# A fused add and layer norm on one core: sums kept in the residual's ring, loops over fixed rows, branch hints, a new transfer order

## The chip, the cores and the metric

The kernel runs on 1 core of one Trainium2 chip. The metric is the device time of one execution in microseconds (us), lower is better. The kernel before takes 238.18 us (median of 3 runs, 238.14 to 238.33). "Span" is what the profile covers of a run, about 1.3 us less than the time.

## The reference

```python
# x, residual: 16 x 1024 x 512, float32; gamma, beta: 512
z = x + residual
mean = np.mean(z, axis=-1, keepdims=True)
var = np.var(z, axis=-1, keepdims=True)
return gamma * (z - mean) / np.sqrt(var + eps) + beta
```

Every element is read twice (x and residual) and written once: 67.11 MB in, 33.55 MB out. The arithmetic is small. In the kernel's words there are 128 "rows": one row is a tile of 128 partitions x 512 elements, 2 KB in each partition.

## The kernel before

Four engines form a pipeline. SyncE issues every large transfer, in the order of a written PLAN, on one queue. GpSimd adds x and residual. ScalarE makes two passes (mean, then sum of squares) and a square root. VectorE makes two passes (add the mean and multiply by gamma; multiply by 1/std and add beta) and a reciprocal between them. x and the result live in a ring of 64 rows (`zbuf`), residual in a ring of 32 rows (`rbuf`). ScalarE and VectorE work in turns of 4 rows.

```python
PLAN = """
x0+8 r0+8 x8+8 r8+8 x16+16 r16+16 x32+16 r32+16
x48+16 r48+16 o0+16 r64+16 x64+16 o16+16 r80+16 x80+16
o32+16 r96+16 x96+8 x104+8 o48+16 r112+16 x112+8 x120+8
o64+16 o80+16 o96+16 o112+12 o124+4
"""                            # r48+16: residual rows 48 to 63; o: a store
ADDS = [4, 4, 8] * 7 + [4] * 4
# ...
for kind, lo, n in moves:      # SyncE, in the order of PLAN
    if kind == "x":
        # ... waits until the store that used these rows of zbuf has landed
    elif kind == "r":
        wait_rows(s_add, "add", lo + n - R_ROWS)   # ring free once ADDED
    else:
        wait_rows(s_out, "out", lo + n)
# GpSimd
z = part(zbuf, Z_ROWS, lo, n)
nc.gpsimd.tensor_tensor(out=z, in0=z, in1=part(rbuf, R_ROWS, lo, n), op=ALU.add
                        ).then_inc(s_add, n)
# ScalarE: 16 laps of 2 turns, addresses from registers
with act.Fori(0, total // LAP) as lap:
    z0 = act.snap((lap * (LAP * D)) % (Z_ROWS * D))
    # ... per turn: wait for the adds, 4 x Identity with accum_out (mean),
    #     4 x Square with accum_out, one Sqrt
# VectorE: 16 laps of 2 turns
    dve.wait_ge(s_ssq, due)    # 4 x (z + nm) * gamma, then wait for std,
                               # reciprocal, 4 x z * rstd + beta
```

Of the kernel before, what the change touches and what calls it, by code (L numbers as in the profile page):

```python
# [8 lines left out]
FP32 = mybir.dt.float32  # L9
ACT = mybir.ActivationFunctionType  # L10
ALU = mybir.AluOpType
# [3 lines left out]
Z_ROWS = 64  # L15
R_ROWS = 32


PLAN = """
x0+8 r0+8 x8+8 r8+8 x16+16 r16+16 x32+16 r32+16  # L20
x48+16 r48+16 o0+16 r64+16 x64+16 o16+16 r80+16 x80+16
o32+16 r96+16 x96+8 x104+8 o48+16 r112+16 x112+8 x120+8
o64+16 o80+16 o96+16 o112+12 o124+4
"""


ADDS = [4, 4, 8] * 7 + [4] * 4


TURN = 4  # L30
SETS = 2
LAP = SETS * TURN


EARLY = 2
# [3 lines left out]
def kernel(  # L39
# [9 lines left out]
    nc = tc.nc  # L49
    P = nc.NUM_PARTITIONS  # L50
# [3 lines left out]
    N, D = xf.shape  # L54
    inv_d = 1.0 / float(D)
    total = N // P
# [16 lines left out]
    def dram(t, lo, n):  # L73

        b0 = lo - lo % BLOCK
        v = t[P * b0 : P * (b0 + BLOCK), :].rearrange("(p j) d -> p j d", p=P)
        return v[:, lo - b0 : lo - b0 + n, :].rearrange("p a b -> p (a b)")

    zbuf = nc.alloc_sbuf_tensor("zbuf", [P, Z_ROWS * D], FP32)
    rbuf = nc.alloc_sbuf_tensor("rbuf", [P, R_ROWS * D], FP32)  # L80
# [1 line left out]
    ones = nc.alloc_sbuf_tensor("ones", [1, P], FP32)  # L82
    eps_t = nc.alloc_sbuf_tensor("eps_t", [P, 1], FP32)
    nm, ssq, std, rstd = (
        [nc.alloc_sbuf_tensor(f"{name}{j}", [P, TURN], FP32) for j in range(SETS)]
        for name in ("nm", "ssq", "std", "rstd")
    )
    gamma_p = nc.alloc_psum_tensor("gamma_p", [P, D], FP32)
    beta_p = nc.alloc_psum_tensor("beta_p", [P, D], FP32)
# [8 lines left out]
    def sem(name):  # L98
        s = nc.alloc_semaphore(name)
        sems.append(s)  # L100
        return s
# [4 lines left out]
    s_gb = [sem(f"gb{k}") for k in range(2)]  # L106
    s_const = sem("const")
    s_pe = sem("pe")
    s_add = sem("add")

    s_mean, s_ssq, s_std = sem("mean"), sem("ssq"), sem("std")
    s_dve = sem("dve")
    s_out = sem("out")
    so = [sem(f"so{c}") for c in range(len(stores))]
    nums = [s.num for s in sems]
# [2 lines left out]
    def part(buf, size, lo, n):  # L118
        assert lo % size + n <= size
        return buf[:, (lo % size) * D : (lo % size + n) * D]  # L120
# [13 lines left out]
        ).then_inc(s_pe, 1)  # L134


    seen = {"add": 0, "out": 0}
    first = []

    def wait_rows(s, key, rows):  # L140
        if rows > seen[key]:
            nc.sync.wait_ge(s, rows)
            seen[key] = rows

    def move(out, in_, s):
        i = nc.sync.dma_start(out=out, in_=in_).then_inc(s, 16)  # L146
        if len(first) < EARLY:
            first.append(i.ins)

    gone = 0  # L150
    for kind, lo, n in moves:
        if kind == "x":
            while gone < len(stores) and stores[gone][0] < lo + n - Z_ROWS:
                nc.sync.wait_ge(so[gone], 16)
                gone += 1
            move(part(zbuf, Z_ROWS, lo, n), dram(xf, lo, n), sx[loads_x.index((lo, n))])
        elif kind == "r":
            wait_rows(s_add, "add", lo + n - R_ROWS)
            move(part(rbuf, R_ROWS, lo, n), dram(rf, lo, n), sr[loads_r.index((lo, n))])
        else:  # L160
            wait_rows(s_out, "out", lo + n)
            move(dram(of, lo, n), part(zbuf, Z_ROWS, lo, n), so[stores.index((lo, n))])


# [8 lines left out]
    lo = 0  # L173
    for n in ADDS:
        for key, loads, s in (("x", loads_x, sx), ("r", loads_r, sr)):
            while landed[key] < len(loads) and loads[landed[key]][0] < lo + n:
                nc.gpsimd.wait_ge(s[landed[key]], 16)  # L177
                landed[key] += 1
        z = part(zbuf, Z_ROWS, lo, n)
        nc.gpsimd.tensor_tensor(  # L180
            out=z, in0=z, in1=part(rbuf, R_ROWS, lo, n), op=ALU.add
        ).then_inc(s_add, n)
        lo += n
    assert lo == total




    act = nc.scalar
    act.preload_act_table_set("sqrt_and_others")  # L190
    act.wait_ge(s_const, 2)
    act.sem_inc(s_dve, LAP)
    with act.Fori(0, total // LAP) as lap:  # L193
        z0 = act.snap((lap * (LAP * D)) % (Z_ROWS * D))
        r0 = act.snap(lap * LAP)
        for j in range(SETS):
            due = act.snap(r0 + (j + 1) * TURN)
            act.wait_ge(s_dve, due)
            act.wait_ge(s_add, due)
            zk = [zbuf[:, bass.ds(z0 + (j * TURN + k) * D, D)] for k in range(TURN)]  # L200
            for k in range(TURN):
                i = act.activation(  # L202
                    out=junk_m[k][:, :],
                    in_=zk[k],
                    func=ACT.Identity,
                    scale=-inv_d,
                    accum_out=nm[j][:, k : k + 1],
                )
            i.then_inc(s_mean, TURN)
            act.wait_ge(s_mean, due)  # L210
            for k in range(TURN):
                i = act.activation(  # L212
                    out=junk_s[k][:, :],
                    in_=zk[k],
                    func=ACT.Square,
                    bias=nm[j][:, k : k + 1],
                    accum_out=ssq[j][:, k : k + 1],
                )
            i.then_inc(s_ssq, TURN)
            act.wait_ge(s_ssq, due)  # L220
            act.activation(  # L221
                out=std[j][:, :],
                in_=ssq[j][:, :],
                func=ACT.Sqrt,
                bias=eps_t[:, 0:1],
                scale=inv_d,
            ).then_inc(s_std, TURN)


    dve = nc.vector  # L230
    dve.wait_ge(s_pe, 2)
    with dve.Fori(0, total // LAP) as lap:
        z0 = dve.snap((lap * (LAP * D)) % (Z_ROWS * D))
        r0 = dve.snap(lap * LAP)
        for j in range(SETS):
            due = dve.snap(r0 + (j + 1) * TURN)
            zk = [zbuf[:, bass.ds(z0 + (j * TURN + k) * D, D)] for k in range(TURN)]
            dve.wait_ge(s_ssq, due)
            for k in range(TURN):
                dve.scalar_tensor_tensor(  # L240
                    out=zk[k],
                    in0=zk[k],
                    scalar=nm[j][:, k : k + 1],
                    in1=gamma_p[:, :],
                    op0=ALU.add,
                    op1=ALU.mult,
                )
            dve.wait_ge(s_std, due)
            dve.reciprocal(out=rstd[j][:, :], in_=std[j][:, :]).then_inc(s_dve, TURN)  # L249
            dve.wait_ge(s_dve, due + LAP)  # L250
            for k in range(TURN):
                i = dve.scalar_tensor_tensor(  # L252
                    out=zk[k],
                    in0=zk[k],
                    scalar=rstd[j][:, k : k + 1],
                    in1=beta_p[:, :],
                    op0=ALU.mult,
                    op1=ALU.add,
                )
            i.then_inc(s_out, TURN)  # L260


    blks = nc.main_func.blocks
# [43 lines left out]
```

## Time and profile before

The first thing to ask is which resource never rests. The page's busy view cuts the span into 40 slices; a digit is the busy share in tenths, 9 is 90% or more.

```profile
DVE  0001977939699999999898989896989895698920
ACT  2019879497999999999999998979998956999300
POOL 0098920999799699604995059944995049950000
DMA  8999999999999999999999999999999999999996
```

The DMA row has 9 everywhere but in the first and the last slice. The table of DMA queues (packets, MB, share of 16 engines' span) says the same in one number, and shows one instruction fetch:

```profile
q1 hardware_dynamic: 4176, 100.67, 99.2%
q14 instruction: 1, 0.01, 0.0%
```

The chain of work that ended last, by engine, is mostly DMA:

```profile
DMA 71%; POOL 9%; ACT 9%; DVE 2%; issue 2%; SPq 1%; ACTq 0%; DVEq 0%; POOLq 0%
```

The groups of instructions (count | busy us, mean ns | idle before, and what ended it) show that the compute engines wait:

```profile
L180 POOL TENSOR_TENSOR zbuf<-zbuf,rbuf 128x2048 f32<-128x2048 f32 (+1 forms) x25 | 142.8, 5740 | 67.6 <-DMA zbuf<-in_x_dram 40.8
L240 DVE SCALAR_TENSOR_TENSOR zbuf<-zbuf,nm,gamma_p 128x512 f32 x128 | 87.1, 743 | 46.3 <-ACT junk_s L212 46.3
L202 ACT ACTIVATE junk_m<-zbuf 128x512 f32 x128 | 74.9, 585 | 29.1 <-POOL zbuf L180 27.5
```

The waits of the queue that issues (SyncE; us in total, times, longest) tell what each transfer's issue hangs on. Here residual loads wait for GpSimd's adds (the first line):

```profile
SPq L146 <- POOL zbuf L180: 94.0, 6, 27.6
SPq L146 <- DMA out_dram<-zbuf: 74.0, 4, 21.0
SPq L146 <- DVE zbuf L252: 46.0, 3, 22.0
```

These waits cost nothing by themselves. What matters is whether the queue still holds issued work when they end. The view of DMA issues (count, KB each, median us from issue to landing) shows that it does: a 4 MB residual load lands 30.5 us after its issue, although the queue lands a 4 MB transfer every 9.7 us (the median engine reports one at 31.49 us and the next at 41.21); it queues behind others.

```profile
rbuf<-in_residual_dram SPq DMA_DIRECT2D x7, 4096.0 KB, 30.5
```

From the timeline of SyncE (start us, duration), the issues of residual rows 32 and 48, and of the last store:

```profile
31.01 0.33 SPq L146 DMA_DIRECT2D rbuf<-in_residual_dram  x1
...
59.41 0.33 SPq L146 DMA_DIRECT2D rbuf<-in_residual_dram  x1
...
226.67 0.33 SPq L146 DMA_DIRECT2D out_dram<-zbuf  x1
```

Where do the 236.9 us of the span go, then? The trace has a record of every DMA packet. A packet of 32 KB (one partition's 16 rows) typically takes 1,213 ns, one of 16 KB 611 ns, one of 8 KB 309 ns. Summed at these values, an engine's data packets take 233.2 us (total of all packets, divided by 16). 16 packets of 32 KB in 1,213 ns are 432 GB/s; what sets this rate is not shown.

### The profile page before, as it was taken

The page shows a single profiled execution, that of the slowest core. Times are in us where ns is not written, and L with a number is a line of the kernel's source. Part 1 is how long each engine was busy: PE and PEld are TensorE (multiplying, and loading weights), DVE is VectorE, ACT ScalarE, POOL GpSimd, SP SyncE. Part 2 cuts the span into 40 slices and gives each one's busy share as a digit, 9 for nine tenths or more (in the row PEclk, how much of TensorE's full clock was granted, in tenths as well). Part 3 has the DMA queues.
Part 4 walks back from the last instruction along what each step waited for, and adds up shares of the span by engine and source line. Part 5 has one row for each costly group of instructions (what it writes and reads, how often), then busy time and mean ns, then how long its engine had stood idle before and what let it go on. Part 6 is the DMA issues. An engine that isn't in the chain of part 4 may idle for free.

```text
span 236.9 us, 1471 instructions
## 1 busy us (share of the span) xinstructions
PE 3.7 (2%) x4; PEld 1.2 (0%) x4; DVE 177.2 (75%) x290; ACT 185.5 (78%) x545; POOL 143.0 (60%) x29
## 2 busy tenths in 40 slices
PE   0600000000000000000000000000000000000000
PEld 0100000000000000000000000000000000000000
DVE  0001977939699999999898989896989895698920
ACT  2019879497999999999999998979998956999300
POOL 0098920999799699604995059944995049950000
DMA  8999999999999999999999999999999999999996
GB/s 310 443 432 426 426 443 443 443 443 443 426 415 398 443 443 443 426 420 409 431 437 443 443 443 432 420 407 429 443 437 437 409 432 448 437 420 437 426 430 285
DMA packets 4181, 100.68 MB, mean 425 GB/s; under 512 B 466, under 2 KB 466, under 8 KB 468
## 3 DMA queue, kind: packets, MB, share of 16 engines
q1 hardware_dynamic: 4176, 100.67, 99.2%
q14 instruction: 1, 0.01, 0.0%
q10 hardware_dynamic: 4, 0.00, 0.0%
HBM read 67.11 MB, written 33.55 MB: 425 GB/s over the span
## 4 chain that ended last, share of the span: by engine, by line
DMA 71%; POOL 9%; ACT 9%; DVE 2%; issue 2%; SPq 1%; ACTq 0%; DVEq 0%; POOLq 0%
DMA out_dram<-zbuf 49%; DMA rbuf<-in_residual_dram 16%; POOL zbuf L180 9%; DMA zbuf<-in_x_dram 6%; ACT junk_s L212 5%; ACT junk_m L202 4%; SPq L146 1%; DVE zbuf L240 1%; DVE zbuf L252 1%; ACTq L202 0%; DVEq L240 0%; ACT std L221 0%; DVE rstd L249 0%; ACTq L193 0%; POOLq L177 0%
## 5 line engine op out<-in xcount | busy, mean ns | idle before, releaser
L180 POOL TENSOR_TENSOR zbuf<-zbuf,rbuf 128x2048 f32<-128x2048 f32 (+1 forms) x25 | 142.8, 5740 | 67.6 <-DMA zbuf<-in_x_dram 40.8
L240 DVE SCALAR_TENSOR_TENSOR zbuf<-zbuf,nm,gamma_p 128x512 f32 x128 | 87.1, 743 | 46.3 <-ACT junk_s L212 46.3
L202 ACT ACTIVATE junk_m<-zbuf 128x512 f32 x128 | 74.9, 585 | 29.1 <-POOL zbuf L180 27.5
L212 ACT ACTIVATE junk_s<-zbuf,nm 128x512 f32 x128 | 88.8, 694 | 1.0
L252 DVE SCALAR_TENSOR_TENSOR zbuf<-zbuf,rstd,beta_p 128x512 f32 x128 | 87.1, 743 | 1.1
L212 ACT ACTIVATION_READ_ACCUMULATOR junk_s<-zbuf,nm 128x1 f32 x128 | 23.9, 187 | 0.0
L202 ACT ACTIVATION_READ_ACCUMULATOR junk_m<-zbuf 128x1 f32 x128 | 23.9, 187 | 0.0
L221 ACT ACTIVATE std<-ssq,eps_t 128x4 f32<-128x4 f32 x32 | 9.5, 297 | 3.0
L249 DVE RECIPROCAL rstd<-std 128x4 f32<-128x4 f32 x32 | 5.5, 170 | 0.0
L190 ACT ACT_TABLE_LOAD x1 | 1.3, 1283 | 2.7 <-PEq L60 2.7
L132 PE MATMUL gamma_p<-gb_row,ones 1*128 1x512 f32 x2 | 2.0, 1119 | 7.2 <-DMA gb_row<-in_gamma_dram 7.2
L132 PE MATMUL beta_p<-gb_row,ones 1*128 1x512 f32 x2 | 1.9, 1052 | 0.0
L127 DVE MEMSET ones<- 1x128 f32 x1 | 0.2, 165 | 2.0 <-PEq L60 2.0
L132 PEld LDWEIGHTS beta_p<-gb_row,ones 1*128 1x128 f32 x2 | 0.7, 328 | 1.0 <-issue 0.5
L132 PEld LDWEIGHTS gamma_p<-gb_row,ones 1*128 1x128 f32 x2 | 0.5, 308 | 7.1 <-issue 7.1
L288 POOL MEMSET const-float32-0.0<- 128x1 f32 x1 | 0.1, 98 | 0.2 <-issue 0.2
L288 POOL MEMSET const-bfloat16-1.0<- 128x1 bf16 x1 | 0.1, 101 | 0.0
L288 POOL MEMSET const-uint8-127<- 128x1 uint8 x1 | 0.1, 101 | 0.0
L288 POOL MEMSET const-float32-1.0<- 128x1 f32 x1 | 0.1, 98 | 0.0
L128 DVE MEMSET eps_t<- 128x1 f32 x1 | 0.1, 59 | 0.0
## 6 DMA issues: line engine op xcount, KB each, us to landing
rbuf<-in_residual_dram SPq DMA_DIRECT2D x7, 4096.0 KB, 30.5
out_dram<-zbuf SPq DMA_DIRECT2D x7, 4096.0 KB, 28.6
zbuf<-in_x_dram SPq DMA_DIRECT2D x5, 4096.0 KB, 28.9
zbuf<-in_x_dram SPq DMA_DIRECT2D x6, 2048.0 KB, 14.9
rbuf<-in_residual_dram SPq DMA_DIRECT2D x2, 2048.0 KB, 15.7
out_dram<-zbuf SPq DMA_DIRECT2D x1, 3072.0 KB, 13.5
out_dram<-zbuf SPq DMA_DIRECT2D x1, 1024.0 KB, 10.2
gb_row<-in_gamma_dram ACTq DMA_DIRECT2D x1, 2.0 KB
```

Of the source, the lines that this page charges most:

```text
L127: nc.vector.memset(ones[:, :], 1.0).then_inc(s_const, 1)
L132: nc.tensor.matmul(dest[:, :], ones[:, :], gb_row[:, k * D : (k + 1) * D], start=True, stop=True).then_inc(s_pe, 1)
L146: i = nc.sync.dma_start(out=out, in_=in_).then_inc(s, 16)
L180: nc.gpsimd.tensor_tensor(out=z, in0=z, in1=part(rbuf, R_ROWS, lo, n), op=ALU.add).then_inc(s_add, n)
L190: act.preload_act_table_set("sqrt_and_others")
L202: i = act.activation(out=junk_m[k][:, :], in_=zk[k], func=ACT.Identity, scale=-inv_d, accum_out=nm[j][:, k : k + 1],)
L212: i = act.activation(out=junk_s[k][:, :], in_=zk[k], func=ACT.Square, bias=nm[j][:, k : k + 1], accum_out=ssq[j][:, k : k + 1],)
L221: act.activation(out=std[j][:, :], in_=ssq[j][:, :], func=ACT.Sqrt, bias=eps_t[:, 0:1], scale=inv_d,).then_inc(s_std, TURN)
L240: dve.scalar_tensor_tensor(out=zk[k], in0=zk[k], scalar=nm[j][:, k : k + 1], in1=gamma_p[:, :], op0=ALU.add, op1=ALU.mult,)
L249: dve.reciprocal(out=rstd[j][:, :], in_=std[j][:, :]).then_inc(s_dve, TURN)
L252: i = dve.scalar_tensor_tensor(out=zk[k], in0=zk[k], scalar=rstd[j][:, k : k + 1], in1=beta_p[:, :], op0=ALU.mult, op1=ALU.add,)
L288: nc = _bacc.Bacc("TRN2", target_bir_lowering=False, num_devices=1)
```

## The change

The intent, as the diff shows it: GpSimd writes the sum into the residual's ring instead of over x. With sums at 32 fixed places, ScalarE's loop can cover the whole ring (8 turns, 4 laps, no address arithmetic), and VectorE's the 64 rows of `zbuf` (16 turns, 2 laps). Each turn gets semaphores of its own, each loop a branch hint (a mark set at the loop's head and attached to its closing branch). The price is that a residual load may overwrite its rows only after VectorE has read the sum, so its wait moves from the add to VectorE's reciprocal, and PLAN is reordered.

```diff
 PLAN:
-x48+16 r48+16 o0+16 r64+16 x64+16 o16+16 r80+16 x80+16
-o32+16 r96+16 x96+8 x104+8 o48+16 r112+16 x112+8 x120+8
-o64+16 o80+16 o96+16 o112+12 o124+4
+x48+16 o0+16 r48+16 o16+16 x64+16 r64+16 x80+16 o32+16 r80+16
+x96+16 r96+16 o48+8 o56+8 r112+8 x112+8 r120+8 x120+8
+o64+16 o80+16 o96+16 o112+8 o120+4 o124+4
-ADDS = [4, 4, 8] * 7 + [4] * 4
+ADDS = [4] * 32
@@ SyncE, residual loads
-            wait_rows(s_add, "add", lo + n - R_ROWS)
+            if lo + n > R_ROWS:
+                last = (lo + n - R_ROWS) // TURN - 1
+                nc.sync.wait_ge(s_rstd[last % Z_TURNS], last // Z_TURNS + 1)
@@ GpSimd
-        z = part(zbuf, Z_ROWS, lo, n)
+        z = part(rbuf, R_ROWS, lo, n)
         nc.gpsimd.tensor_tensor(
-            out=z, in0=z, in1=part(rbuf, R_ROWS, lo, n), op=ALU.add
-        ).then_inc(s_add, n)
+            out=z, in0=part(zbuf, Z_ROWS, lo, n), in1=z, op=ALU.add
+        ).then_inc(s_sum[lo // TURN % R_TURNS], 1)
@@ ScalarE (VectorE alike, over Z_ROWS)
-    with act.Fori(0, total // LAP) as lap:
-        z0 = act.snap((lap * (LAP * D)) % (Z_ROWS * D))
+    with act.Fori(0, total // R_ROWS) as lap:
+        hints.append(act.mark_branch_hint_location())
@@ VectorE, first pass
-            dve.wait_ge(s_ssq, due)
+            dve.wait_ge(s_std[j % R_TURNS], due[j // R_TURNS])
-                    out=zk[k], in0=zk[k], ...
+                    out=part(zbuf, Z_ROWS, r, 1), in0=part(rbuf, R_ROWS, r, 1), ...
# (semaphore tables and address helpers cut)
```

More of the change, by code (lines that the diff above doesn't have):

```diff
@@ L19 @@
 PLAN = """
-x0+8 r0+8 x8+8 r8+8 x16+16 r16+16 x32+16 r32+16
-x48+16 r48+16 o0+16 r64+16 x64+16 o16+16 r80+16 x80+16
-o32+16 r96+16 x96+8 x104+8 o48+16 r112+16 x112+8 x120+8
-o64+16 o80+16 o96+16 o112+12 o124+4
+x0+8 r0+8 x8+8 r8+8 x16+16 r16+16 x32+16 r32+16 x48+16
+o0+16 r48+16 o16+16 x64+16 r64+16 x80+16 o32+16 r80+16
+x96+16 r96+16 o48+8 o56+8 r112+8 x112+8 r120+8 x120+8
+o64+16 o80+16 o96+16 o112+8 o120+4 o124+4
 """
-ADDS = [4, 4, 8] * 7 + [4] * 4
+ADDS = [4] * 32
 TURN = 4
-SETS = 2
-LAP = SETS * TURN
+R_TURNS = R_ROWS // TURN
+Z_TURNS = Z_ROWS // TURN
 EARLY = 2
@@ L84 @@
     nm, ssq, std, rstd = (
-        [nc.alloc_sbuf_tensor(f"{name}{j}", [P, TURN], FP32) for j in range(SETS)]
-        for name in ("nm", "ssq", "std", "rstd")
+        nc.alloc_sbuf_tensor(name, [P, R_ROWS], FP32) for name in ("nm", "ssq", "std", "rstd")
     )
@@ L108 @@
     s_pe = sem("pe")
-    s_add = sem("add")
-    s_mean, s_ssq, s_std = sem("mean"), sem("ssq"), sem("std")
-    s_dve = sem("dve")
+    s_sum, s_mean, s_ssq, s_std = (
+        [sem(f"{name}{j}") for j in range(R_TURNS)] for name in ("sum", "mean", "ssq", "std")
+    )
+    s_rstd = [sem(f"rstd{j}") for j in range(Z_TURNS)]
     s_out = sem("out")
@@ L134 @@
         ).then_inc(s_pe, 1)
-    seen = {"add": 0, "out": 0}
+    seen = 0
     first = []
-    def wait_rows(s, key, rows):
-        if rows > seen[key]:
-            nc.sync.wait_ge(s, rows)
-            seen[key] = rows
     def move(out, in_, s):
@@ L157 @@
         elif kind == "r":
-            wait_rows(s_add, "add", lo + n - R_ROWS)
+            if lo + n > R_ROWS:
+                last = (lo + n - R_ROWS) // TURN - 1
+                nc.sync.wait_ge(s_rstd[last % Z_TURNS], last // Z_TURNS + 1)
             move(part(rbuf, R_ROWS, lo, n), dram(rf, lo, n), sr[loads_r.index((lo, n))])
         else:
-            wait_rows(s_out, "out", lo + n)
+            if lo + n > seen:
+                nc.sync.wait_ge(s_out, lo + n)
+                seen = lo + n
             move(dram(of, lo, n), part(zbuf, Z_ROWS, lo, n), so[stores.index((lo, n))])
@@ L178, with column @@
                 landed[key] += 1
-        z = part(zbuf, Z_ROWS, lo, n)
+        z = part(rbuf, R_ROWS, lo, n)
         nc.gpsimd.tensor_tensor(
-            out=z, in0=z, in1=part(rbuf, R_ROWS, lo, n), op=ALU.add
-        ).then_inc(s_add, n)
+            out=z, in0=part(zbuf, Z_ROWS, lo, n), in1=z, op=ALU.add
+        ).then_inc(s_sum[lo // TURN % R_TURNS], 1)
         lo += n
     assert lo == total
+    def column(t, lo, n=1):
+        return t[:, lo % R_ROWS : lo % R_ROWS + n]
+    hints = []
     act = nc.scalar
@@ L191 @@
     act.wait_ge(s_const, 2)
-    act.sem_inc(s_dve, LAP)
-    with act.Fori(0, total // LAP) as lap:
-        z0 = act.snap((lap * (LAP * D)) % (Z_ROWS * D))
-        r0 = act.snap(lap * LAP)
-        for j in range(SETS):
-            due = act.snap(r0 + (j + 1) * TURN)
-            act.wait_ge(s_dve, due)
-            act.wait_ge(s_add, due)
-            zk = [zbuf[:, bass.ds(z0 + (j * TURN + k) * D, D)] for k in range(TURN)]
-            for k in range(TURN):
+    with act.Fori(0, total // R_ROWS) as lap:
+        hints.append(act.mark_branch_hint_location())
+        due = act.snap(lap + 1)
+        for j in range(R_TURNS):
+            rows = range(j * TURN, (j + 1) * TURN)
+            act.wait_ge(s_sum[j], due)
+            for k, r in enumerate(rows):
                 i = act.activation(
                     out=junk_m[k][:, :],
-                    in_=zk[k],
+                    in_=part(rbuf, R_ROWS, r, 1),
                     func=ACT.Identity,
                     scale=-inv_d,
-                    accum_out=nm[j][:, k : k + 1],
+                    accum_out=column(nm, r),
                 )
-            i.then_inc(s_mean, TURN)
-            act.wait_ge(s_mean, due)
-            for k in range(TURN):
+            i.then_inc(s_mean[j], 1)
+            act.wait_ge(s_mean[j], due)
+            for k, r in enumerate(rows):
                 i = act.activation(
                     out=junk_s[k][:, :],
-                    in_=zk[k],
+                    in_=part(rbuf, R_ROWS, r, 1),
                     func=ACT.Square,
-                    bias=nm[j][:, k : k + 1],
-                    accum_out=ssq[j][:, k : k + 1],
-                )
-            i.then_inc(s_ssq, TURN)
-            act.wait_ge(s_ssq, due)
+                    bias=column(nm, r),
+                    accum_out=column(ssq, r),
+                )
+            i.then_inc(s_ssq[j], 1)
+            act.wait_ge(s_ssq[j], due)
             act.activation(
-                out=std[j][:, :],
-                in_=ssq[j][:, :],
+                out=column(std, rows[0], TURN),
+                in_=column(ssq, rows[0], TURN),
                 func=ACT.Sqrt,
@@ L226 @@
                 scale=inv_d,
-            ).then_inc(s_std, TURN)
+            ).then_inc(s_std[j], 1)
     dve = nc.vector
     dve.wait_ge(s_pe, 2)
-    with dve.Fori(0, total // LAP) as lap:
-        z0 = dve.snap((lap * (LAP * D)) % (Z_ROWS * D))
-        r0 = dve.snap(lap * LAP)
-        for j in range(SETS):
-            due = dve.snap(r0 + (j + 1) * TURN)
-            zk = [zbuf[:, bass.ds(z0 + (j * TURN + k) * D, D)] for k in range(TURN)]
-            dve.wait_ge(s_ssq, due)
-            for k in range(TURN):
+    with dve.Fori(0, total // Z_ROWS) as lap:
+        hints.append(dve.mark_branch_hint_location())
+        due = [dve.snap(lap * 2 + 1), dve.snap(lap * 2 + 2)]
+        turn = dve.snap(lap + 1)
+        for j in range(Z_TURNS):
+            rows = range(j * TURN, (j + 1) * TURN)
+            dve.wait_ge(s_std[j % R_TURNS], due[j // R_TURNS])
+            for r in rows:
                 dve.scalar_tensor_tensor(
-                    out=zk[k],
-                    in0=zk[k],
-                    scalar=nm[j][:, k : k + 1],
+                    out=part(zbuf, Z_ROWS, r, 1),
+                    in0=part(rbuf, R_ROWS, r, 1),
+                    scalar=column(nm, r),
                     in1=gamma_p[:, :],
@@ L247 @@
                 )
-            dve.wait_ge(s_std, due)
-            dve.reciprocal(out=rstd[j][:, :], in_=std[j][:, :]).then_inc(s_dve, TURN)
-            dve.wait_ge(s_dve, due + LAP)
-            for k in range(TURN):
+            dve.reciprocal(
+                out=column(rstd, rows[0], TURN), in_=column(std, rows[0], TURN)
+            ).then_inc(s_rstd[j], 1)
+            dve.wait_ge(s_rstd[j], turn)
+            for r in rows:
+                z = part(zbuf, Z_ROWS, r, 1)
                 i = dve.scalar_tensor_tensor(
-                    out=zk[k],
-                    in0=zk[k],
-                    scalar=rstd[j][:, k : k + 1],
+                    out=z,
+                    in0=z,
+                    scalar=column(rstd, r),
                     in1=beta_p[:, :],
@@ L260 @@
             i.then_inc(s_out, TURN)
+    loops = [b for b in nc.main_func.blocks if b.name.endswith("_loop")]
+    for b, hint in zip(loops, hints):
+        bass.BassInstruction(b.instructions[-1]).branch_hint(hint)
     blks = nc.main_func.blocks
```

## The prediction

> **What bounds the kernel now.** The DMA engines, from end to end. The page's busy slices show DMA at 9 in all slices but the first and last; the queue table shows one queue at 99.2% of 16 engines' span for 100.67 MB. The trace's packet records show no gap: a 32 KB packet takes 1,213 ns (432 GB/s for 16 engines), a 16 KB one 611, an 8 KB one 309; at these values all data packets come to 233.2 us per engine, of a 236.9 us span. The rest: 1.0 us before the first packet, 0.7 of slow first packets, 0.4 of slow packets near 77 us, about 1 us of engines that finish early at the end. [...] ScalarE (78% busy), VectorE (75%) and GpSimd (60%) wait for data; the chain of waits is 71% DMA.
>
> **What the change does, costed.**
> - Bytes: the same. Transfers become 18 of 16 rows, 11 of 8, 2 of 4 (before: 19, 8, one of 12, one of 4): 233.38 us of packets instead of 233.25, plus two 9 ns semaphore writes per engine.
> - GpSimd: 8-row adds (8.9 us) become two of 4 rows (4.5 us): same work, earlier release of ScalarE (its wait for GpSimd is 27.5 us now). Off the critical path.
> - ScalarE, VectorE: address computations and most loop heads go (16 laps become 4 and 2). The timeline shows them nearly hidden: a ScalarE turn is 5.85 us, with some 0.2 us more at a lap head. Perhaps 2 us of ScalarE in all, off the path.
> - The residual ring's release moves from the add to VectorE's reciprocal: later by a ScalarE turn (5.85 us) plus a VectorE pass (2.85 us), plus queueing.
>
> I worked out (an estimate) every transfer's issue and end by recurrence from trace durations: 9.76 us per 16-row transfer, adds 4.5, ScalarE turns 5.85, VectorE 2.85+2.75. For the kernel before it gives nearly every issue within 1 us and the DMA end at 236.0 (trace 236.4). For the change, the first waiting residual load is issued at 43 us instead of 31, the next at 72 instead of 59, and ScalarE ends at 223 instead of 221. Yet the DMA backlog stays positive at every issue: about 6 us at the tightest ring loads, 3.5 us at the last store. DMA end: +0.2 us. So neither ScalarE's and VectorE's saving nor the longer release lies on the critical path; slack in the queue is spent instead.
>
> **Prediction.** 238.4 us, 237.7 to 239.3. Faster by over 2%: 1%; within 2%: 97%; slower: 2%.
>
> **What would show it.** DMA still 9 in all slices, near 99%; residual loads' issue-to-landing much shorter (30.5 us median now, towards 17 to 22); DMA queue waits for VectorE's reciprocal in place of GpSimd's adds; ScalarE's idle before its mean pass falls; packet times unchanged; last store issued near 229 us instead of 226.7, still behind queued stores.
>
> **What would make it wrong.** [...] This trace has one instruction packet (8 KB, 309 ns). A stall of over 3 us at ScalarE's last lap head, where it runs back to back, would leave DMA dry at the last store; many fetches on one DMA engine would delay that engine's end. A faster result would need less skew among engines at the end, worth under 1 us.

Two passages are cut from this text: a bandwidth limit, and a rule about instruction fetches. Its sum: 238.2 us of before plus 0.2 us at the DMA's end make 238.4 us. The stall of over 3 us that it names is the author's estimate, set against the 3.5 us of backlog.

## The result, and the profile after

The changed kernel takes 238.03 us (median of 4 runs, 237.89 to 238.24); the kernel before took 238.22 us in the same session. The ratio is 0.9992, with a 95% interval from 0.9975 to 1.0010: the same. Ratios here are the mean time of one kernel's fast runs over that of the other's of the same rounds, so not quite the ratio of the medians that are quoted.

The busy view after, the same rows of it that matter:

```profile
ACT  2019997299999996999909998099999999999600
DMA  8999999999999999999999999999999999999997
```

The queue table: 288 packets more, the same bytes, the same one instruction fetch.

```profile
q1 hardware_dynamic: 4464, 100.67, 99.4%
q14 instruction: 1, 0.01, 0.0%
```

The groups: GpSimd's adds are now all of one shape. ScalarE's wait for GpSimd has not fallen; it rose from 27.5 to 33.7 us.

```profile
L178 POOL TENSOR_TENSOR rbuf<-zbuf,rbuf 128x2048 f32<-128x2048 f32 x32 | 143.7, 4521 | 62.2 <-DMA rbuf<-in_residual_dram 60.0
L201 ACT ACTIVATE junk_m<-rbuf 128x512 f32<-128x512 f32 x128 | 74.2, 580 | 34.0 <-POOL rbuf L178 33.7
```

SyncE's waits: the residual loads now wait for VectorE's reciprocal, 131.6 us in all, where they waited 94.0 us for the adds.

```profile
SPq L140 <- DVE rstd L247: 131.6, 7, 38.5
SPq L140 <- DVE zbuf L253: 50.6, 7, 22.9
SPq L140 <- DMA out_dram<-zbuf: 32.9, 4, 17.9
```

The timeline of SyncE: the same three issues as above come 11.8, 12.6 and 1.6 us later. And the view of DMA issues shows what paid for it: the residual loads spend less time in the queue.

```profile
42.77 0.33 SPq L140 DMA_DIRECT2D rbuf<-in_residual_dram  x1
...
72.01 0.33 SPq L140 DMA_DIRECT2D rbuf<-in_residual_dram  x1
...
228.23 0.33 SPq L140 DMA_DIRECT2D out_dram<-zbuf  x1
```

```profile
rbuf<-in_residual_dram SPq DMA_DIRECT2D x6, 4096.0 KB, 21.2
```

The chain view changed its face: ScalarE now leads it.

```profile
ACT 48%; DMA 35%; POOL 6%; DVE 4%; issue 1%; SPq 1%; ACTq 0%; DVEq 0%; POOLq 0%
```

A reader may take this for a kernel that ScalarE bounds. It is not, and experiments 3 and 4 show it. The chain is followed back from the last instruction, which is a VectorE pass of the last rows. It does not know that the store of these rows then sat in a queue that was full anyway.

How much issued work still stood in the queue at an issue (its backlog) can be read from the traces: the time from a transfer's issue to the median engine's report that the transfer ahead of it has landed. It fell from 19.9 to 8.1 us for residual rows 32, from 10.9 to 8.6 us for rows 48, and from 6.7 to 5.0 us for the last store. (A transfer that found the queue empty, in experiment 1, had its first packet 1.0 us after its issue, so that much of the figure is needed.) This is the slack that the change spends. It does not run out: the smallest backlog of all issues after the first seven is 5.0 us, where it was 5.2 us before, at the last store but one.

From the packet records, us per engine (sums over 16 engines, divided by 16):

| | before | after |
|---|---|---|
| data packets at typical durations | 233.25 | 233.38 |
| what packets took beyond that | 1.56 | 1.50 |
| of it in the first 5 us | 0.74 | 0.69 |
| of it between 60 and 83 us | 0.43 | 0.45 |
| engines idle after 235 us (early finishers) | 1.04 | 0.73 |

The estimated +0.13 us of more and smaller packets is there, and the ends vary by more than that. Nothing else moved.

### The profile page after: what moved, and what is told of

Same layout as the page of the kernel before. It is cut to its first block, busy times and chain, and to the rows that moved or that the text cites. A ratio compares the mean times of both kernels' runs of the same rounds, so it can differ in the third digit from the quotient of the medians.

```text
span 236.7 us, 1000 instructions
## 1 busy us (share of the span) xinstructions
PE 3.8 (2%) x4; PEld 1.2 (0%) x4; DVE 177.2 (75%) x290; ACT 183.8 (78%) x545; POOL 144.0 (61%) x36
## 3 DMA queue, kind: packets, MB, share of 16 engines
q1 hardware_dynamic: 4464, 100.67, 99.4%
## 4 chain that ended last, share of the span: by engine, by line
ACT 48%; DMA 35%; POOL 6%; DVE 4%; issue 1%; SPq 1%; ACTq 0%; DVEq 0%; POOLq 0%
DMA rbuf<-in_residual_dram 35%; ACT junk_s L211 25%; ACT junk_m L201 21%; POOL rbuf L178 6%; DVE zbuf L239 3%; ACT std L220 2%; DVE zbuf L253 1%; SPq L140 1%; DVE rstd L247 0%; ACTq L194 0%; DVEq L231 0%; POOLq L175 0%; ACTq L199 0%; ACTq L195 0%
## 5 line engine op out<-in xcount | busy, mean ns | idle before, releaser
L178 POOL TENSOR_TENSOR rbuf<-zbuf,rbuf 128x2048 f32<-128x2048 f32 x32 | 143.7, 4521 | 62.2 <-DMA rbuf<-in_residual_dram 60.0
L239 DVE SCALAR_TENSOR_TENSOR zbuf<-rbuf,nm,gamma_p 128x512 f32<-128x512 f32 x128 | 87.1, 743 | 47.8 <-ACT std L220 47.8
L201 ACT ACTIVATE junk_m<-rbuf 128x512 f32<-128x512 f32 x128 | 74.2, 580 | 34.0 <-POOL rbuf L178 33.7
L211 ACT ACTIVATE junk_s<-rbuf,nm 128x512 f32<-128x512 f32 x128 | 88.8, 694 | 1.0
L253 DVE SCALAR_TENSOR_TENSOR zbuf<-zbuf,rstd,beta_p 128x512 f32<-128x512 f32 x128 | 87.1, 744 | 1.1
L211 ACT ACTIVATION_READ_ACCUMULATOR junk_s<-rbuf,nm 128x1 f32 x128 | 23.9, 187 | 0.0
L201 ACT ACTIVATION_READ_ACCUMULATOR junk_m<-rbuf 128x1 f32 x128 | 23.8, 186 | 0.0
## 6 DMA issues: line engine op xcount, KB each, us to landing
rbuf<-in_residual_dram SPq DMA_DIRECT2D x6, 4096.0 KB, 21.2
```

What stands on the lines that cost most here:

```text
L178: nc.gpsimd.tensor_tensor(out=z, in0=part(zbuf, Z_ROWS, lo, n), in1=z, op=ALU.add).then_inc(s_sum[lo // TURN % R_TURNS], 1)
L201: i = act.activation(out=junk_m[k][:, :], in_=part(rbuf, R_ROWS, r, 1), func=ACT.Identity, scale=-inv_d, accum_out=column(nm, r),)
L211: i = act.activation(out=junk_s[k][:, :], in_=part(rbuf, R_ROWS, r, 1), func=ACT.Square, bias=column(nm, r), accum_out=column(ssq, r),)
L239: dve.scalar_tensor_tensor(out=part(zbuf, Z_ROWS, r, 1), in0=part(rbuf, R_ROWS, r, 1), scalar=column(nm, r), in1=gamma_p[:, :], op0=ALU.ad ...
L253: i = dve.scalar_tensor_tensor(out=z, in0=z, scalar=column(rstd, r), in1=beta_p[:, :], op0=ALU.mult, op1=ALU.add,)
```

## The experiments

Theory 1: the DMA queue is full from end to end, so ScalarE's and VectorE's savings are worth nothing; the later release of the residual ring would cost time, but the new order hides it. Rival A: ScalarE bounds the changed kernel (the chain view). Rival B: large gains and losses cancel, for example a better order against a later release. Rival C: the hints or the loops are worth time on their engines. Twelve kernels were run, each timed in 3 rounds. Three give a wrong result on purpose; the others were correct. GpSimd's work was varied in none of them.

### 1. The old order under the new release (a_old_order)

```diff
 # on the changed kernel
-PLAN = (new order)
+PLAN = (the order of before)
```

> The changed kernel with the transfer order of before. Theory 1 (the later release of the residual ring is only harmless because the new order puts a store ahead of the load that waits): by the recurrence with trace durations the DMA queue runs dry twice, about 3.0 us before the load of residual rows 48 to 63 and 3.5 us before rows 64 to 79; time about 244.4 us (6.3 more). Theory 2 (the queue has slack enough in any order): 238.0 to 238.5 us, no gap in the packets.

Measured: 246.32 us (246.25 to 246.41), ratio 1.0337 (1.0320 to 1.0354). Theory 2 of that text falls. The view by windows (us; busy and count of PE, PEld, DVE, ACT, POOL; clock, DMA share, GB/s) shows the two holes:

```profile
70.00:73.00 3.00, 0.00 (x0) 0.00 (x0) 2.96 (x6) 2.97 (x11) 3.00 (x2) 1.00 0.00 0
94.00:96.30 2.30, 0.00 (x0) 0.00 (x0) 2.27 (x5) 2.27 (x7) 2.30 (x2) 1.00 0.00 0
```

The DMA moves nothing while all three compute engines work. The load of residual rows 48 is issued at 72.07 us, as late as in the changed kernel (72.01), but here nothing stands in the queue before it: its turn came at 70 us. The packet records give 3.4 and 2.2 us of idle engines for the two holes, against an expected 3.0 and 3.5. The rest of the 8.3 us is a cost that the expectation had left out: slow packets. They took 4.41 us per engine beyond their typical durations instead of 1.50. The first packets after a hole took up to 2.07 us instead of 1.21 (1.2 us per engine for both holes), and the last ones of the two loads that have the first two stores behind them up to 2.37 us (2.2 us per engine near 82 and 115 us; the changed kernel lost 0.4 us as its first store came up). So 5.6 us of holes and 2.9 us of slow packets make up about the difference, and the new order is worth about 8 us to the changed kernel.

### 2. The new order alone (b_new_order)

```diff
 # on the kernel before
-PLAN = (the order of before)
+PLAN = (new order)
```

> The kernel before with the new transfer order alone. Theory 1 (DMA bound, the order only makes room for the later release): 238.2 us, within 0.3 us of before, DMA busy all the time. Rival (the new order is itself a gain that the later release takes back): about 6 us faster, 232 us.

Measured: 238.55 us (238.42 to 239.11), ratio 1.0018 (1.0001 to 1.0034). The rival's 6 us of gain are not there; if anything it is 0.2% slower: 0.24 us over the 238.31 of the kernel before in the same session, inside the stated 0.3. Experiments 1 and 2 together: the order is worth nothing while the ring is freed early, and 8 us when it is freed late. It is not a gain; it makes room for the release.

### 3. Without the mean pass (a_cut_mean)

```diff
-                i = act.activation(out=junk_m[k][:, :], in_=part(rbuf, R_ROWS, r, 1),
-                    func=ACT.Identity, scale=-inv_d, accum_out=column(nm, r))
-            i.then_inc(s_mean[j], 1)
-            act.wait_ge(s_mean[j], due)
+    nc.vector.memset(nm[:, :], 0.0).then_inc(s_const, 1)   # once; wrong result on purpose
```

> The changed kernel without ScalarE's mean pass (128 activations of 580 ns and their accumulator reads go; the result is wrong on purpose). Theory 1 (DMA bound): 238.0 us within 0.3, although ScalarE's busy time falls from 184 to about 122 us. Rival (ScalarE, which the chain of the changed kernel gives 48% of the span, is what bounds it): clearly faster, by over 5 us.

Measured: 237.89 us (237.80 to 238.10), against 238.03 for the changed kernel in another session; 0.9981 of before (0.9964 to 0.9998). ScalarE's busy time fell from 183.8 us to the following (the page's busy line; the expectation of 122 counted overlapping instructions twice), and the time stayed. Rival A falls.

```profile
PE 3.7 (2%) x4; PEld 1.2 (0%) x4; DVE 174.9 (74%) x291; ACT 104.6 (44%) x289; POOL 143.9 (61%) x36
```

### 4. One store fewer, with and without the mean pass (a_less_store, a_less_store_cut_mean)

```diff
-o64+16 o80+16 o96+16 o112+8 o120+4 o124+4
+o80+16 o96+16 o112+8 o120+4 o124+4          # rows 64 to 79 stay unwritten, on purpose
```

> The changed kernel without the store of rows 64 to 79, 4.2 MB or 9.76 us of packets fewer (wrong result on purpose). Theory 1 (DMA bound, with the compute chain close behind): falls by about 4.7 us only, to 233.4, since the last store then waits for ScalarE and VectorE. Pure DMA: 228.3 us. Compute bound: no change.

> Both cuts: no store of rows 64 to 79 and no mean pass. Theory 1: with ScalarE out of the way the whole 9.76 us come back, about 228.5 us (8.9 to 9.8 less than the changed kernel), against 233.4 with the store's cut alone and 238.0 with the pass's cut alone.

Measured: 233.41 us (233.39 to 233.47) and 228.07 us (227.96 to 228.21). The first hit; the second came 0.4 us below the 228.5 that was told, 9.96 us less than the changed kernel where at most 9.8 was told. The store is 9.76 us of packets; taking it away gives 4.6 us back (238.03 less 233.41), then the last stores wait for compute and the DMA share falls. This is the window of the last 8 us of the first of the two:

```profile
224.00:232.00 8.00, 0.00 (x0) 0.00 (x0) 4.10 (x7) 0.00 (x0) 0.00 (x0) 1.00 0.52 214
```

With the mean pass gone too, the whole 9.96 us come back. So cutting bytes pays at once, cutting ScalarE's work pays nothing, and after 4.6 us of bytes ScalarE's work pays again. That is how far the second limit stands behind the first.

### 5. More work on VectorE (a_dve_more, b_dve_more)

```diff
+            dve.scalar_tensor_tensor(out=spare[1][:, :], in0=spare[0][:, :],
+                scalar=column(nm, rows[0]), in1=gamma_p[:, :], op0=ALU.add, op1=ALU.mult)
             dve.reciprocal(...)
```

> The changed kernel with one more VectorE pass of 128x512 (about 0.7 us) per turn ahead of the reciprocal, into a spare tile. Theory 1 (slack in the queue was spent: the changed kernel has less to spare than before): VectorE is then the slowest engine, the last store is issued after the queue is empty; about 240.0 us (2 more). Rival (both kernels have the same slack): same time as the changed kernel, or the same loss as its twin on the kernel before.

> The kernel before with the same extra VectorE pass per turn. Theory 1: hidden, 238.2 us, as the recurrence leaves about 4 us of backlog at the last store. Rival: as above.

Measured: 238.28 us (238.11 to 238.56) and 238.24 us (238.13 to 238.38); both ratios are 1.0003. The twin behaved as told; the expected 240.0 us for the changed kernel did not come. VectorE did become the slowest engine; the timeline shows its last pass ending at 233.3 us, where the last store is issued:

```profile
230.37 0.17 DVE L258 RECIPROCAL rstd<-std 128x4 f32<-128x4 f32 x1
230.58 2.72 DVE L264 SCALAR_TENSOR_TENSOR zbuf<-zbuf,rstd,beta_p 128x512 f32<-128x512 f32 x4
```

Two things were mis-sized. The turn was 6.14 us, not the 6.3 that the sum gave. And a hole of 0.89 us per engine did open before the last store, but most engines had that time to lose. The transfer is split over 16 DMA engines, and the trace has the time at which each of them reported its part of the last store. In the changed kernel the median engine reports at 235.69 us and the slowest at 236.62, 0.92 later; with the extra pass the median reports at 237.09 and the slowest at 237.19. After the late start the slowest engine is 0.10 us behind the median, no longer 0.92. The changed kernel has less to spare than before, as theory 1 says: its last store has no backlog left here, its twin's still has. But the hole of 0.89 us is covered by the engines' spread of 0.92 us, so the times don't tell the two apart.

### 6. The hints (a_no_hint, a_no_hint_2, a_nop, a_hint_act, a_hint_dve)

```diff
 # a_no_hint, a_no_hint_2 (the same text, built and loaded anew)
-        hints.append(act.mark_branch_hint_location())
-        hints.append(dve.mark_branch_hint_location())
 # a_nop: in place of each hint, two no-operations
+        act.nop(nofuse=True)
 # a_hint_act, a_hint_dve: one of the two hints stays
```

> The changed kernel without the two branch hints. Theory 1: time 238.0 us, within 0.3 us, whatever the hints do, as ScalarE has about 4 us to spare at the last store. Question beside it: ScalarE's pause at its three lap heads was 0.17 to 0.2 us with the hint[...]; if not, the pauses stay at 0.2 us.

No effect on the time was expected, and there was one. Measured: 240.00 us (239.84 to 240.11), ratio 1.0068 (1.0052 to 1.0085). The place that one would suspect is innocent: in the view of waits ScalarE's mean pass had two pauses of "issue", 0.4 us in all, with the hints, and has none without. The DMA queue's table and the window of the last 2.6 us show what happened:

```profile
q14 instruction: 2, 0.02, 0.0%
```

```profile
236.20:238.80 2.60, 0.00 (x0) 0.00 (x0) 0.00 (x0) 0.00 (x0) 0.00 (x0) 1.00 0.05 22
```

There are two instruction fetches now, and in the last 2.6 us the 16 DMA engines are busy for 5%, less than the share of one of them. The packet records place the two fetches, 8 KB each, at 32.2 and 46.8 us, and a data packet right after each took 1.59 and 1.88 us instead of 1.21. The reports of the 16 engines show the rest. The lag of the slowest behind the median engine is 0.12 us at 31.7 us, 0.53 in the next transfer, 0.89 at 51.9 us, then 2.25 at 92.6 us and 2.84 at the end. The packets can be chained to engines, as each starts within some ns of the end of the one before it (3 to 4 ns in the traces of the kernel before and the changed kernel). Chained so, the two fetches lie on two different engines: the 0.53 is the engine of the first fetch, the 0.89 that of the second. The second one is the engine that ends last, at 238.4 us; the first ends at 236.2, among the others (235.1 to 236.3). In this trace each engine moved a sixteenth of the bytes (chained, 6.29 MB of the 100.67 in all), and the one that fell behind stayed behind (the lag is 2.25 us at 92.6 us and still 2.25 at 160.5); the last packets are its own, and the span ends 0.4 us after them, at 238.8.

Two explanations were left for the two early fetches: the hints are missing, or the two removed instructions shifted the code. The last four kernels were for that.

> The changed kernel with two no-operations in place of each hint, so that the code behind keeps about its place. Hint theory [...]: about 240.0 us, the slowest engine's landing of the last store 2 to 3 us behind the median one. Layout rival (only the code's place matters): 238.0 us, 0.9 us behind.

> The changed kernel with ScalarE's hint alone. If ScalarE's hint is the one that counts: 238.0 us and one instruction packet; if VectorE's: 240.0 us and two packets before 50 us; if each is worth a part: about 239.

> The changed kernel with VectorE's hint alone: the other half of the same question (238.0, 240.0 or about 239 us).

> The kernel without hints again, word for word, built and loaded anew. If its 2 us belong to the kernel: 239.8 to 240.2 us, and the same lag of one DMA engine that begins near 32 and 47 us; if they belonged to that one loading: 238.0 us.

| kernel | time us (range) | ratio to before (95%) | 8 KB fetches at us | lag of the slowest engine, last store, us |
|---|---|---|---|---|
| before | 238.18 (238.14 to 238.33) | 1 | 225.4 | 1.15 |
| changed, both hints | 238.03 (237.89 to 238.24) | 0.9992 (0.9975 to 1.0010) | 202.4 | 0.92 |
| a_hint_dve | 238.61 (238.24 to 239.32) | 1.0020 (0.9999 to 1.0042) | 32.0, 202.6 | 0.79 |
| a_hint_act | 239.66 (239.47 to 239.81) | 1.0053 (1.0036 to 1.0070) | 47.9, 204.9 | 2.34 |
| a_no_hint | 240.00 (239.84 to 240.11) | 1.0068 (1.0052 to 1.0085) | 32.2, 46.8 | 2.84 |
| a_no_hint_2 | 239.66 (239.47 to 239.90) | 1.0057 (1.0041 to 1.0074) | 33.2, 46.7 | 2.34 |
| a_nop | 239.85 (239.33 to 240.09) | 1.0055 (1.0038 to 1.0072) | 33.3, 46.8 | 3.09 |

The loss comes back in a second build, so it belongs to the kernel. No-operations don't mend it, which speaks against the layout. Without ScalarE's hint there is a fetch near 32 us, without VectorE's one near 47 us. VectorE's is the one that counts: with its hint alone the time is within 0.4% of before, without it 0.5 to 0.7% slower, whatever ScalarE has. In each of the four kernels without it, the engine that carried the fetch near 47 us is the one that ends last. (a_hint_dve's four runs spread from 238.24 to 239.32, and its lag in the table is from the fastest of them; whether ScalarE's hint is worth anything stays open. The kernel before took 238.31 and 238.39 us in the sessions of these runs.) Rival C is right that the hints are worth time, and wrong about where: not on their engines, but, as these traces suggest, on the DMA engine that carries the fetch.

What stays open: a fetch (309 ns in the traces of the kernel before and the changed kernel) and the slowed packet after it (1.88 us instead of 1.21) account for the lag up to about 0.9 us. It then grows to 1.4 to 2.6 us until 90 us, while the first stores pass through the queue. The growth is in slow packets of that same engine: between 66 and 72 us they took 1.0 to 1.2 us beyond their typical durations in the four kernels (the median engine's 0.5 to 0.8), and between 86 and 92 us another 0.5 to 1.0 us (the median engine's nothing). Why this engine's packets are slowed more than the others' is not explained. Nor did any run move the fetch alone, so that the fetch starts the lag is read from the order of events in four traces; that the missing hint costs the time is shown.

### A version that beats both

No run was made for one, and the sums say why. Data packets at their typical durations are 233.4 us per engine and the first starts at 1.0 us; that makes 234.4 us, an estimate from the packet records, and the last packet of the changed kernel ends at 236.1 us. At these packet times at most 1.7 us (0.7%) are left without moving fewer bytes, in slow first packets and in the spread of the engines.

## Why the prediction was right or wrong, point by point

- "What bounds the kernel now. The DMA engines": right. A store less saves 4.6 us, ScalarE's mean pass less saves nothing, both together save 10.0.
- Time: 238.4 us was told with 237.7 to 239.3, 238.03 was measured. The predicted +0.2 us is below what the runs resolve.
- "Packet times unchanged", DMA near 99%, residual loads' time in the queue towards 17 to 22 us: right (1,213, 611 and 309 ns; 99.4%; 21.2 us).
- "The first waiting residual load is issued at 43 us instead of 31, the next at 72 instead of 59", last store near 229: right (42.8, 72.0, 228.2). The recurrence needs only durations and the order of the waits, and it also showed which order leaves the queue empty; a_old_order's two holes were foretold within 1.3 us each. It has no term for slow packets (2.9 us more there).
- "Slack in the queue is spent instead": right in mechanism. But the text did not say that the order was what kept the slack; it listed the transfers by size only. Experiments 1 and 2 show that the order is the part that decides, worth about 8 us. The backlog stayed positive at the issues where it was told to: 7.9 us at the tightest ring loads and 5.0 us at the last store, 1.0 us of each being needed, against about 6 and 3.5 told.
- "ScalarE's idle before its mean pass falls": wrong. It rose from 29.1 to 34.0 us. The step that failed is "earlier release of ScalarE" by the smaller adds: the new order puts stores ahead of residual loads, so rows arrive later, and ScalarE waits for them (about 6 us each near 118 and 147 us in its gaps). The trace of b_new_order settles it: there the new order alone, with the larger adds kept, raises ScalarE's wait for GpSimd from 27.5 to 33.3 us. It costs nothing, for the same reason as everything else.
- "Perhaps 2 us of ScalarE in all": right in size; its busy time fell from 185.5 to 183.8 us.
- What would make it wrong: the text feared "a stall of over 3 us at ScalarE's last lap head". No trace here shows such a stall: ScalarE's pauses of "issue" before its mean pass are 0.4 us in all with the hints, the longest 0.2, and none without (view of waits). Its other fear, "many fetches on one DMA engine would delay that engine's end", is near to what was measured without VectorE's hint, but many were not needed: the engine that ends last carried a single extra fetch of 8 KB, and its lag was 0.8 to 0.9 us after it and 2.3 to 3.1 us at the end. That the fetch is the cause was not shown.

## What to carry to other kernels

When one DMA queue is busy all the time, ask of a change only what it does to the bytes and to the backlog at each issue: follow every transfer's wait and end with durations from the trace, and the order of the queue turns out to be the part that can cost 8 us while the compute savings are worth none. A buffer that is freed later needs something else to stand ahead of the load that waits for it (in a_old_order nothing did, and the DMA stood still for 3.4 and 2.2 us). And look at the engines one by one at the end: in the seven kernels of experiment 6's table the slowest of the 16 engines reported the last store 0.8 to 3.1 us after the median one, so look for what set that engine back. Here leaving out VectorE's branch hint cost 1.6 to 2 us (239.66 to 240.00 against 238.03), and in all four traces without it the engine that ended last had carried an extra 8 KB instruction fetch near 47 us.
